# A hybrid decoder trunk on one core: two priorities in the scheduler that orders the instructions

## The chip, the core and the metric

One of the eight cores of a Trainium2 chip runs the whole program. Its engines work side by side, each through its own instructions in a fixed order: TensorE (PE) for matrix products, VectorE (DVE), ScalarE (ACT), GpSimd (POOL), and SyncE (SP), which here only issues DMAs. An instruction that waits for another engine holds everything behind it on its own engine. The metric is the device time of one execution in microseconds, lower is better.

## The reference, cut to what matters

Two layers over 256 tokens of width 1024, all in float32:

```
h = rmsnorm(x, norm_mix)
aq, ak, av, iq, ik, iw, hq, hf, hi, hg, ga, gb = split(h @ w_in)
y_attn = dsa_attention(rope(rmsnorm(aq)), rope(rmsnorm(ak)), av, rope(iq), rope(ik), iw)   # top 64 of 256 keys by an indexer score
o      = hgrn2_chunked(silu(hq), 1 - f, hi, log f)          # f from sigmoid(hf)
y_hgrn = rmsnorm(o) * silu(hg)
merged = sigmoid(ga) * (y_attn @ w_proj_attn) + sigmoid(gb) * (y_hgrn @ w_proj_hgrn)
x = x + merged @ w_out
g, u = split(rmsnorm(x, norm_ffn) @ w_ffn_in)
x = x + (silu(g) * u) @ w_ffn_out
```

The weights are read once. The result is x after the second layer.

## The kernel before

**Products.** A product in float32 is made of three in a shorter format. Each operand is split into a rounded part hi and the rest lo, and hi·hi, hi·lo and lo·hi are added up in PSUM (`mm3`). All weights come in 69 chunks per layer, nearly all of 128 x 2048 elements (1 MB). `take()` fetches the next one: a DMA on SP into a tile w, ACT writes hi as a rounded copy, DVE writes lo = w - hi. There are three buffers each for w, hi and lo, so a chunk's hi can begin once the chunk three before it has been used up by PE. A group of 512 output columns (`group`) takes two such chunks and 48 products of 128x512.

**Order of a layer.** The groups of `w_in` come as idx, aq, ak, hf, hq, av, vh, hg, ga, gb, ga, gb. In between lies the vector work of the attention: `ev_idx` and the top-64 search (eight rounds of MAX and MATCH_REPLACE for each of two blocks of 128 queries, i = 0 and 1, on the tile `work`), `ev_qk` (norm and rotation of queries and keys, tiles raw, sq, s, n.., ropet, rot, then a transpose by PE into `qkp` and a copy by ACT into qT or kT), the logits (`lg`, PE), softmax (`lm`, DVE and ACT), and transposes of it (`ptp`, PE). `ev_hf` sends the forget gate through a transpose on PE (`hfp`) and two sigmoids on ACT (fT, KR). After that come the HGRN part (`hd`, `hl`, `hc`, `po`), both projections (`pj`), `out_gemm` for `w_out` (accumulators wo), the gated product (`fi`), and `out_gemm` for `w_ffn_out` (fo).

**`out_gemm`.** The last two chunks are taken together. The four accumulators (token block i, column half g) then end one after another, 12 products each. Behind each: x = x + accumulator (DVE), and `norm_half`: xg = x·g (DVE), four transposes (`xT`, PE), hi on ACT, lo on DVE (tiles h2T, or hT for the next layer), squares on ACT. `norm_scale` turns the sums of squares into 1/rms by Newton steps on DVE, ten tiny instructions per block.

**What sets the order.** Nothing runs where it is written. Every call is recorded, and `Program.schedule` sorts them by simulating the engines in Python with prices for each instruction. An engine that is free takes, of the instructions that could start, the one with the largest `o.tail + o.extra`: the tail is the longest remaining path in ns, the extra is `prog.rank` at the time of recording. So a rank of 2e4 counts like 20 us more of path. The warm-up products (`gate`, of which `WARM` are recorded) have an extra of -1e9 and fill PE's idle time only; the tile `zero` that they read keeps its buffer (tag s2, six buffers for all temporary tiles) until the last of them. All instructions are emitted by one line, so the profile gives line 467 to all of them, and one tells them apart by their tiles.

Of the kernel before, what the change touches and what calls it, by code (L numbers as in the profile page):

```python
# [26 lines left out]
N_IDX = 324  # L27
C_HQ, C_HF, C_HV, C_HG, C_GA, C_GB = 1860, 2372, 2884, 3396, 3908, 4932
FIRST = {(0, C_IDX): 2, (0, C_AQ): 2}
WARM = 28  # L30
LEVELS = (2, 4, 8)
TWO_PI = 2.0 * np.pi

# [444 lines left out]
def hybrid_trunk(prog, x_d, pos_d, w_in, w_pa, w_ph, w_out, n_mix, n_ffn,  # L478
# [7 lines left out]
    def big(name, shape, dt=F32):  # L486
        return prog.tile("s4", shape, dt, name)
# [4 lines left out]
    def small(name, n=16):  # L492
        return prog.tile("sm", [n], F32, name)

    def bank(name, tag="Q"):
        return prog.tile(tag, [512], F32, name)
# [21 lines left out]
                                     for o in (0, DFF)]) + ([4, 512],))  # L518
        add_rows(w_fo, l, 2, 1024, 0)

    state = {"used": 0}

    def take():
        c = state["used"]
        state["used"] += 1
        a, b, kn = chunks[c]
        k, n = kn or b
        wt, ht, lt = "w" if k * n > 1024 else "s4", "hi", "lo"
        w = prog.tile(wt, [k, n], F32, f"w{c}")
        hi = prog.tile(ht, [k, n], F32R, f"hi{c}")  # L530
        lo = prog.tile(lt, [k, n], F32R, f"lo{c}")
        prog.rank = 5e5 - 1e3 * c
        if kn is None:
            SP.dma_start(w, a)
        else:
            SP.dma_start(w[:, :, 0:256], a)
            SP.dma_start(w[:, :, 256:512], b)
        prog.rank = 0.0
        S.activation(hi, w, AF.Copy)
        V.tensor_tensor(lo, w, hi.bitcast(F32), op=ALU.subtract)  # L540
        return hi, lo

    def mm3(acc, h, hk, wc, wk, wsl, start, stop):

        hh, hl = h
        wh, wl = wc
        with prog.one(main=True):
            PE.matmul(acc, hh[:, hk, :], wh[:, wk, wsl], start=start, stop=False)
            PE.matmul(acc, hh[:, hk, :], wl[:, wk, wsl], start=False, stop=False)
            PE.matmul(acc, hl[:, hk, :], wh[:, wk, wsl], start=False, stop=stop)  # L550
# [32 lines left out]
    gate = bank("gate")  # L583
    for _ in range(WARM):
        PE.matmul(gate[:, 0:256], zero[:, 0:128], zero, start=True, stop=True)
# [15 lines left out]
    def split_to(hi_ap, lo_ap, src, scale=None):  # L601

        if scale is None:
            S.activation(hi_ap, src, AF.Copy)
            V.tensor_tensor(lo_ap, src, hi_ap.bitcast(F32), op=ALU.subtract)
        else:
            S.activation(hi_ap, src, AF.Copy, scale=scale)
            V.scalar_tensor_tensor(lo_ap, src, scale, hi_ap.bitcast(F32), op0=ALU.mult, op1=ALU.subtract)
# [11 lines left out]
    def norm_half(i, g, gkey, hT, ssq, tag):  # L620

        xs = x[:, i, g * 512:(g + 1) * 512]
        pt = bank(f"xT{i}{g}", tag)
        pv = pt.rearrange("p (k t) -> p k t", k=4)
        xg = tmp(f"xg{i}{g}", [512])
        V.tensor_tensor(xg, xs, gbc[gkey][:, g * 512:(g + 1) * 512], op=ALU.mult)
        transpose4(pt, xg)
        split_to(hT[i][0][:, g * 4:g * 4 + 4, :], hT[i][1][:, g * 4:g * 4 + 4, :], pv)
        junk = tmp(f"sq{i}{g}", [512])
        S.activation(junk, xs, AF.Square, accum_out=ssq[:, g:g + 1])  # L630

    def norm_scale(ssq, name):
        t = small(name + "t")
        V.tensor_tensor(t[:, 0:1], ssq[:, 0:1], ssq[:, 1:2], op=ALU.add)
        return newton(t[:, 0:1], 1, 1.0 / D, name)
# [117 lines left out]
    def layer(l, hT, R):  # L753
        last = l == DEPTH - 1
        def group(n, name, evac, kk=4):
            accs = [bank(f"{name}{i}_{l}", "P") for i in range(NT)]
            for c in range(8 // kk):
                wc = take()
                for i in range(NT):
                    for k in range(kk):  # L760
                        kt = c * kk + k
                        mm3(accs[i][:, :n], hT[i], kt, wc, k, slice(0, n), kt == 0, kt == 7)
            for i in range(NT):
                evac(i, accs[i][:, :n])
# [76 lines left out]
        group(512, "ak", ev_qk(1, kT))  # L841


        PT = []
        for i in range(NT):
            W = (i + 1) * 128
            mx, nb, sm, rs = small(f"mx{i}"), small(f"nb{i}"), small(f"sum{i}"), small(f"rs{i}")
            pts = [big(f"PT{i}{j}", [8, 128]) for j in range(i + 1)]
            lms = [big(f"lm{i}{p}", [4, W]) for p in range(2)]
# [13 lines left out]
            for p in range(2):  # L863
# [10 lines left out]
                for j in range(i + 1):  # L874
# [5 lines left out]
                    S.activation(dst, pt.rearrange("p (a t) -> p a t", a=4), AF.Copy)  # L880
            PT.append(pts)

# [41 lines left out]
        for i in range(NT):  # L924
            py = bank(f"py{i}")
            for hp0 in (0, 2):
                with prog.one():
                    for hp in range(hp0, hp0 + 2):
                        for j in range(i + 1):
                            for p in range(2):  # L930
                                h = 2 * hp + p
                                PE.matmul(py[64 * p:64 * p + 64, hp * 128:(hp + 1) * 128], av[:, j, h * 64:(h + 1) * 64],
                                          PT[i][j][:, h, :], start=j == 0, stop=j == i)
            split_to(yT[i][0][:, 0:4, :], yT[i][1][:, 0:4, :], py.rearrange("p (k t) -> p k t", k=4))
# [134 lines left out]
            split_to(yT[i][0][:, 4:8, :], yT[i][1][:, 4:8, :], pv, gc)  # L1069


        gates = {}

        def ev_gate(key):
# [11 lines left out]
        for g in range(2):  # L1086
            ws = [take(), take()]
            for i in range(NT):
                pab = []
                for s in range(2):  # L1090
                    acc = bank(f"pj{s}{i}{g}", "P")
                    for k in range(4):
                        mm3(acc, yT[i], s * 4 + k, ws[s], k, slice(0, 512), k == 0, k == 3)
                    pab.append(acc)
                ma, mb = tmp(f"ma{i}", [512]), tmp(f"mb{i}", [512])
                V.tensor_tensor(ma, pab[0], gates["a" + str(g)][:, i, :], op=ALU.mult)
                V.tensor_tensor(mb, pab[1], gates["b" + str(g)][:, i, :], op=ALU.mult)
                V.tensor_tensor(ma, ma, mb, op=ALU.add)
                pt = bank(f"mp{i}", "Q")
                transpose4(pt, ma)  # L1100
                split_to(mT[i][0][:, g * 4:g * 4 + 4, :], mT[i][1][:, g * 4:g * 4 + 4, :], pt.rearrange("p (k t) -> p k t", k=4))

        def out_gemm(n_chunks, lhs, gkey, hT_out, name):

            accs = [[bank(f"{name}{i}{g}", "Q") for g in range(2)] for i in range(NT)]
            for c in range(n_chunks - 2):
                wc = take()
                for i in range(NT):
                    for k in range(2):
                        (hh, hl), hk = lhs(i, 2 * c + k)  # L1110
                        with prog.one(main=True):
                            for g in range(2):
                                gs = slice(g * 512, (g + 1) * 512)
                                PE.matmul(accs[i][g], hh[:, hk, :], wc[0][:, k, gs], start=c == 0 and k == 0, stop=False)
                                PE.matmul(accs[i][g], hh[:, hk, :], wc[1][:, k, gs], start=False, stop=False)
                            for g in range(2):
                                gs = slice(g * 512, (g + 1) * 512)
                                PE.matmul(accs[i][g], hl[:, hk, :], wc[0][:, k, gs], start=False, stop=False)
            wcs = [take(), take()]
            Rn = []  # L1120
            for i in range(NT):
                ssq = small(f"{name}ss{i}")
                for g in range(2):
                    for c in range(2):
                        for k in range(2):
                            kt = 2 * (n_chunks - 2 + c) + k
                            h, hk = lhs(i, kt)
                            mm3(accs[i][g], h, hk, wcs[c], k, slice(g * 512, (g + 1) * 512), kt == 0, c == 1 and k == 1)
                    xs = x[:, i, g * 512:(g + 1) * 512]
                    V.tensor_tensor(xs, xs, accs[i][g], op=ALU.add)  # L1130
                    if hT_out is not None:
                        norm_half(i, g, gkey, hT_out, ssq, "P")
                    else:
                        SP.dma_start(out_d[0, i * 128:(i + 1) * 128, g * 512:(g + 1) * 512], xs)
                if hT_out is not None:
                    Rn.append(norm_scale(ssq, f"{name}r{i}"))
            return Rn

        h2T = pair(f"h2T{l}")
        R2 = out_gemm(4, lambda i, k: (mT[i], k), f"f{l}", h2T, "wo")  # L1140
        if not last:
            load_g(f"m{l + 1}", n_mix[l + 1])
# [19 lines left out]

        hT_n = None if last else pair(f"hT{l + 1}")
        R_n = out_gemm(11, lambda i, k: ((acts[k // 2][:, i, 0], acts[k // 2][:, i, 1]), k % 2), f"m{l + 1}", hT_n, "fo")
        return hT_n, R_n

    for l in range(DEPTH):
        hT, R = layer(l, hT, R)
# [43 lines left out]
```

## Time and profile before

| | |
|---|---|
| time, median of 3 runs | 814.75 us (814.44 to 815.56) |
| the profiled execution | 815.19 us, of which its span is 813.4 us |
| PE busy | 801.3 us (99%), 3986 products |
| PE weight loads | 657.3 us (81%) |
| DVE busy | 537.6 us (66%) |
| ACT busy | 400.9 us (49%) |
| bytes from HBM | 137.95 MB, 171 GB/s over the span |
| mean granted clock of PE | 0.996 of full speed |

The ends of products are modelled, so a PE that is busy for 99% may still run below its pace. One sees that by the starts: in an undisturbed stretch there are 46 products of 128x512 in 10 us. The chain that ended last lies on PE for 84% and on DVE for 10%, of which the splits (lo) are 4% of the span.

### The profile page before, as it was taken

To read this page: it belongs to the slowest core of one execution; us is meant where nothing else is said; L and a number is where in the kernel's file an instruction comes from. 1 tells how busy PE (TensorE), PEld (TensorE's weight loads), DVE (VectorE), ACT (ScalarE), POOL (GpSimd) and SP (SyncE) were. 2 spreads that over 40 slices of the span, in tenths; PEclk is the share of its full clock that TensorE was granted. 3 is DMA by queue.
4 is the path that set the end of the run, shared out by engine and by line. 5 is a ranking of instruction groups with operands and counts; after the bars stand their busy time and mean duration, and the time that the engine had idled before them with its cause. 6 is when DMAs were issued, how large, how long until landed. Compare 5 with 4: busy or idle time off the path is not lost.

```text
span 813.4 us, 10251 instructions
## 1 busy us (share of the span) xinstructions
PE 801.3 (99%) x3986; PEld 657.3 (81%) x3986; DVE 537.6 (66%) x936; ACT 400.9 (49%) x506; POOL 6.5 (1%) x8
## 2 busy tenths in 40 slices
PE   8989999999999999999999999999999999999998
PEld 7767788888888888888887778888888888888886
DVE  6999856577775455554489997566868645556442
ACT  5764855344364435453356667533445544445330
POOL 3000000000000000000000000000000000000000
PEclk9998999999999999999999999999999999999999
DMA  9725555333656656536546356443354665655531
GB/s 319 248 69 176 186 188 174 104 124 129 219 176 206 195 169 203 170 144 222 168 154 219 111 201 207 155 156 105 108 202 156 206 204 168 199 177 186 169 142 52
DMA packets 86793, 139.66 MB, mean 172 GB/s; under 512 B 3269, under 2 KB 51033, under 8 KB 86745
## 3 DMA queue, kind: packets, MB, share of 16 engines
q1 hardware_dynamic: 86584, 138.94, 51.4%
q8 instruction: 31, 0.51, 0.2%
q14 instruction: 18, 0.14, 0.0%
q10 hardware_dynamic: 160, 0.07, 0.0%
HBM read 137.95 MB, written 1.05 MB: 171 GB/s over the span
## 4 chain that ended last, share of the span: by engine, by line
PE 84%; DVE 10%; issue 2%; ACT 2%; DMA 0%; POOL 0%; POOLq 0%; ACTq 0%; DVEq 0%
PE fi L467 29%; PE fo L467 15%; PE pj L467 5%; PE gb L467 5%; PE wo L467 5%; PE ga L467 4%; DVE lo L467 4%; PE av L467 3%; PE hg L467 3%; PE vh L467 3%; PE hq L467 2%; DVE work L467 2%; PE aq L467 1%; ACT hi L467 1%; PE fp L467 1%
## 5 line engine op out<-in xcount | busy, mean ns | idle before, releaser
L467 DVE TENSOR_TENSOR lo<-w,hi 128x2048 fp32r<-128x2048 f32 (+3 forms) x134 | 296.4, 2212 | 218.5 <-ACT hi L467 217.9
L467 ACT ACTIVATE hi<-w 128x2048 fp32r<-128x2048 f32 (+3 forms) x134 | 247.3, 1846 | 280.7 <-PE fi L467 95.1
L467 PE MATMUL fi<-hi,h2T_hi 128*128 128x512 f32 x352 | 140.8, 400 | 0.2
L467 PE MATMUL fi<-hi,h2T_lo 128*128 128x512 f32 x352 | 137.8, 391 | 0.0
L467 PE MATMUL fi<-lo,h2T_hi 128*128 128x512 f32 x352 | 137.1, 390 | 0.0
L467 PE MATMUL fo<-hi,act 128*128 128x512 f32 x352 | 109.9, 391 | 0.0
L467 PEld LDWEIGHTS fi<-hi,h2T_lo 128*128 128x128 f32 x352 | 66.1, 188 | 15.0 <-DVE h2T_lo L467 0.7
L467 PEld LDWEIGHTS fo<-hi,act 128*128 128x128 f32 x352 | 66.1, 188 | 13.7
L467 PEld LDWEIGHTS fi<-hi,h2T_hi 128*128 128x128 f32 x352 | 66.1, 188 | 13.3 <-DVE h2T_lo L467 0.8
L467 PEld LDWEIGHTS fi<-lo,h2T_hi 128*128 128x128 f32 x352 | 66.2, 188 | 12.6
L467 PE MATMUL fo<-lo,act 128*128 128x512 f32 x176 | 68.5, 389 | 0.0
L467 PEld LDWEIGHTS fo<-lo,act 128*128 128x128 f32 x176 | 33.1, 188 | 6.6
L467 PE MATMUL gb<-hi,hT_hi 128*128 128x512 f32 x64 | 26.7, 418 | 0.0
L467 PE MATMUL wo<-hi,mT_hi 128*128 128x512 f32 x64 | 25.9, 405 | 0.0
L467 PE MATMUL pj<-hi,yT_hi 128*128 128x512 f32 x64 | 25.8, 404 | 0.0
L467 PE MATMUL ga<-hi,hT_hi 128*128 128x512 f32 x64 | 25.7, 401 | 0.0
L467 PE MATMUL wo<-lo,mT_hi 128*128 128x512 f32 x64 | 25.1, 392 | 0.0
L467 PE MATMUL gb<-hi,hT_lo 128*128 128x512 f32 x64 | 25.1, 392 | 0.0
L467 PE MATMUL gb<-lo,hT_hi 128*128 128x512 f32 x64 | 25.0, 391 | 0.0
L467 PE MATMUL ga<-hi,hT_lo 128*128 128x512 f32 x64 | 25.0, 391 | 0.0
L467 PE MATMUL pj<-hi,yT_lo 128*128 128x512 f32 x64 | 25.0, 391 | 0.0
L467 PE MATMUL pj<-lo,yT_hi 128*128 128x512 f32 x64 | 25.0, 390 | 0.0
(340 smaller groups left out, 1302.0 us busy)
## 6 DMA issues: line engine op xcount, KB each, us to landing
w<-in_w_ffn_in_dram SPq DMA_DIRECT2D x88, 512.0 KB, 4.5
w<-in_w_in_dram SPq DMA_DIRECT2D x42, 1024.0 KB, 4.9
w<-in_w_ffn_out_dram SPq DMA_DIRECT2D x22, 1024.0 KB, 4.7
w<-in_w_out_dram SPq DMA_DIRECT2D x8, 1024.0 KB, 4.7
w<-in_w_proj_attn_dram SPq DMA_DIRECT2D x4, 1024.0 KB, 4.9
w<-in_w_proj_hgrn_dram SPq DMA_DIRECT2D x4, 1024.0 KB, 4.8
w<-in_w_in_dram SPq DMA_DIRECT2D x4, 512.0 KB, 4.6
w<-in_w_in_dram SPq DMA_DIRECT2D x4, 324.0 KB, 5.5
```

The costliest lines, as they stand in the source:

```text
L467: getattr(engines[o.eng], name)(*[real(x) for x in a], **{n: real(x) for n, x in k.items()})
```

## The change

```diff
-WARM = 28
+WARM = 24
+AHEAD = 2e4
...
-    state = {"used": 0}
+    state = {"used": 0, "ahead": 0.0}
...
-        prog.rank = 0.0
+        prog.rank = state["ahead"]
         S.activation(hi, w, AF.Copy)
         V.tensor_tensor(lo, w, hi.bitcast(F32), op=ALU.subtract)
+        prog.rank = 0.0
...
         group(512, "ak", ev_qk(1, kT))
+        state["ahead"] = AHEAD
...
             split_to(yT[i][0][:, 4:8, :], yT[i][1][:, 4:8, :], pv, gc)
+        state["ahead"] = 0.0
...
+                    prog.rank = AHEAD
                     xs = x[:, i, g * 512:(g + 1) * 512]
                     V.tensor_tensor(xs, xs, accs[i][g], op=ALU.add)
                     if hT_out is not None:
                         norm_half(i, g, gkey, hT_out, ssq, "P")
                     else:
                         SP.dma_start(out_d[0, i * 128:(i + 1) * 128, g * 512:(g + 1) * 512], xs)
+                    prog.rank = 0.0
```

From the group hf up to hg, both halves of the split of a weight chunk get 20 us of priority. In `out_gemm` the addition to x, the scaled copy, its transposes, its split and the squares get the same. Four warm-up products are dropped. No computation changes; PE has four products fewer, ACT loads its function table 14 times where it did 10 times, SP swaps one small load (the vector for the FFN's norm) with a weight chunk.

VectorE, layer 0, around the split of the first chunk of hq (`lo_800` before, `lo_669` now; work is the top-64 search, n00 the Newton steps of the first query block's norm, ropet a key's rotation). Before:

```order
L467 TENSOR_TENSOR n00a<-n00a,n00v 128x8
L467 TENSOR_TENSOR ropet<-raw_622,rs_775 128x8x32
L467 SCALAR_TENSOR_TENSOR n00y<-n00a,n00y 128x8
L467 TENSOR_TENSOR lo_800<-w_516,hi_648 128x2048
L467 SCALAR_TENSOR_TENSOR n00a<-n00y 128x8
L467 MAX m_812<-work_580 128x8
```

And now:

```order
L468 SCALAR_TENSOR_TENSOR work_630<-rel_628,iw_490,work_630 128x256
L468 MATCH_REPLACE work_606<-m_653,work_606 128x128
L468 MAX m_660<-work_630 128x8
L468 MAX m_667<-work_606 128x8
L468 TENSOR_TENSOR lo_669<-w_520,hi_641 128x2048
L468 MATCH_REPLACE work_606<-m_667,work_606 128x128
L468 MATCH_REPLACE work_630<-m_660,work_630 128x256
```

The split stood behind the whole search but two rounds and behind most of the query norm, as the 153rd instruction of VectorE; now it stands at the beginning of the search, as the 109th. 44 instructions have gone behind it, none has come ahead of it.

TensorE, layer 0, from the end of the group hf to the start of hq (hfp: transposes of the forget gate, qkp: of a rotated query or key). Before:

```order
L467 MATMUL qkp_750<-ident,rot_718 128x128 x4
L467 MATMUL hf_0_687<-hi_578,hT_hi_214 128x512
L467 MATMUL hf_0_687<-lo_694,hT_hi_214 128x512
L467 MATMUL hf_0_687<-hi_578,hT_lo_230 128x512
...
L467 MATMUL hfp_777<-ident,hfraw_748 128x128 x4
L467 MATMUL hfp_804<-ident,hfraw_796 128x128 x4
L467 MATMUL hq_0_815<-hi_648,hT_hi_206 128x512
L467 MATMUL hq_0_815<-lo_800,hT_hi_206 128x512
```

And now, first at the same place and then where the first hfp has gone, in the group vh:

```order
L468 MATMUL hf_0_673<-lo_587,hT_hi_215 128x512
L468 MATMUL hf_0_673<-hi_558,hT_lo_231 128x512
L468 MATMUL hq_0_743<-hi_641,hT_hi_207 128x512
L468 MATMUL hq_0_743<-lo_669,hT_hi_207 128x512
...
L468 MATMUL vh_0_1004<-hi_927,hT_lo_221 128x512
L468 MATMUL ptp_1108<-ident,lm_1010 128x128 x4
L468 MATMUL hfp_1114<-ident,hfraw_793 128x128 x4
L468 MATMUL vh_0_1004<-hi_927,hT_hi_207 128x512
```

No transpose stands between hf and hq any more. The second query block's qkp has gone 27 products into hq, both keys' qkp into av and vh, the logits lg from hq and av into av and vh, and the second hfp right behind the first transpose of hq's own gate, in the first group gb. Layer 1 is moved likewise.

TensorE, end of the product with `w_out` (wo_2031 before and wo_2028 now are the last accumulator, i = 1 and g = 1; 12 products each). Before:

```order
L467 MATMUL wo_2030<-hi_2050,mT_lo_1998 128x512
L467 MATMUL xT_2122<-ident,xg_2102 128x128 x4
L467 MATMUL wo_2031<-hi_1970,mT_hi_1985 128x512
...
L467 MATMUL wo_2031<-hi_1970,mT_lo_1998 128x512
L467 MATMUL xT_2145<-ident,xg_2109 128x128 x4
L467 MATMUL wo_2031<-hi_2050,mT_hi_1985 128x512
...
L467 MATMUL xT_2164<-ident,xg_2135 128x128 x4
L467 MATMUL fi_2173<-hi_2063,h2T_hi_2132 128x512
```

And now:

```order
L468 MATMUL xT_2110<-ident,xg_2099 128x128 x4
L468 MATMUL xT_2119<-ident,xg_2106 128x128 x4
L468 MATMUL wo_2027<-hi_2047,mT_hi_1982 128x512
...
L468 MATMUL xT_2161<-ident,xg_2151 128x128 x4
L468 MATMUL fi_2170<-hi_2060,h2T_hi_2126 128x512
...
L468 MATMUL fi_2170<-hi_2060,h2T_lo_2135 128x512
L468 MATMUL xT_2186<-ident,xg_2177 128x128 x4
L468 MATMUL fi_2170<-hi_2060,h2T_hi_2126 128x512
```

The first two transposes come three and nine products earlier, and the fourth, which came behind 27 products of fi, comes behind six.

## Rows read from the trace of the kernel before

**Rows 1.** Windows: us, busy us (instructions) of PE, PEld, DVE, ACT, POOL, PEclk, DMA
```profile
50.00:60.00 10.00, 6.73 (x34) 4.96 (x33) 10.00 (x34) 7.38 (x9) 0.00 (x0) 0.98 0.32 106
60.00:70.00 10.00, 9.68 (x32) 7.71 (x33) 10.00 (x46) 2.70 (x5) 0.00 (x0) 0.67 0.46 141
240.00:250.00 10.00, 10.00 (x46) 8.28 (x45) 5.37 (x4) 5.79 (x5) 0.00 (x0) 1.00 0.55 186
```

**Rows 2.** Timeline of PE, layer 0: start, us, operation [idle before <-releaser]
```profile
26.64 0.51 PE L467 MATMUL ak<-lo,hT_hi 128*128 128x512 f32 x1 [0.16 <-DVE lo L467]
...
53.00 0.39 PE L467 MATMUL hf<-hi,hT_lo 128*128 128x512 f32 x1
53.56 0.63 PE L467 MATMUL qkp<-ident,rot 128*128 128x128 f32 x4 [0.17 <-DVE rot L467]
53.94 0.48 PE L467 MATMUL hf<-hi,hT_hi 128*128 128x512 f32 x1
...
55.41 0.60 PE L467 MATMUL hfp<-ident,hfraw 128*128 128x128 f32 x4
58.16 0.66 PE L467 MATMUL hfp<-ident,hfraw 128*128 128x128 f32 x4 [2.14 <-ACT hfraw L467]
58.57 0.47 PE L467 MATMUL hq<-hi,hT_hi 128*128 128x512 f32 x1
60.32 0.79 PE L467 MATMUL hq<-lo,hT_hi 128*128 128x512 f32 x1 [1.28 <-DVE lo L467]
...
66.46 0.44 PE L467 MATMUL hq<-hi,hT_hi 128*128 128x512 f32 x1
```

**Rows 3.** Timeline of DVE, layer 0
```profile
46.91 2.27 DVE L467 TENSOR_TENSOR lo<-w,hi 128x2048 fp32r<-128x2048 f32 x1
49.10 0.08 DVE L467 MATCH_VALUE_LOAD work<-m,work 128x8 f32 x1
...
57.98 2.29 DVE L467 TENSOR_TENSOR lo<-w,hi 128x2048 fp32r<-128x2048 f32 x1
...
67.24 0.69 DVE L467 TENSOR_TENSOR rot<-rot,n10y 128x512 f32<-128x512 f32 x1
```

**Rows 4.** DVE groups by form, 24.3 to 58 us: busy us, mean ns, idle before
```profile
L467 DVE MAX8 m<-work 128x8 f32<-128x256 f32 x8 | 3.3, 416 | 0.0
L467 DVE MATCH_REPLACE8 work<-m,work 128x256 f32<-128x256 f32 x8 | 3.3, 407 | 0.0
L467 DVE TENSOR_TENSOR rot<-raw,rc 128x512 f32<-128x512 f32 x3 | 2.0, 678 | 0.0
```

**Rows 5.** Timeline of PE, layer 1
```profile
417.63 0.51 PE L467 MATMUL aq<-lo,hT_hi 128*128 128x512 f32 x1 [0.17 <-DVE lo L467]
...
459.45 0.50 PE L467 MATMUL hq<-lo,hT_hi 128*128 128x512 f32 x1 [0.18 <-DVE lo L467]
...
465.12 0.48 PE L467 MATMUL hq<-hi,hT_hi 128*128 128x512 f32 x1
465.87 0.50 PE L467 MATMUL hq<-lo,hT_hi 128*128 128x512 f32 x1 [0.26 <-DVE lo L467]
```

**Rows 6.** Timeline of PE behind the first product with w_out
```profile
229.15 0.50 PE L467 MATMUL fi<-hi,h2T_lo 128*128 128x512 f32 x1
229.74 0.50 PE L467 MATMUL fi<-hi,h2T_hi 128*128 128x512 f32 x1
```

**Rows 7.** Timeline of ACT, layer 0
```profile
58.12 1.28 ACT L467 ACT_TABLE_LOAD   x1
59.41 0.60 ACT L467 ACTIVATE fT<-hfp 128x512 f32<-128x512 f32 x1
```

**Rows 8.** Timeline of DVE, layer 1, in the first group gb
```profile
531.05 0.18 DVE L467 TENSOR_TENSOR F<-F 128x16 f32<-128x16 f32 x1 [2.58 <-PE hqp L467]
531.93 2.29 DVE L467 TENSOR_TENSOR lo<-w,hi 128x2048 fp32r<-128x2048 f32 x1 [0.70 <-ACT hi L467]
```

## Prediction

> **What bounds the kernel now.** I read the windows first, by the number of products that PE starts in 10 us, because its busy time is modelled. At rest 46 products of 128x512 start in 10 us, 0.227 us apart from start to start, with DVE busy for half of the time [rows 1]. From 50 to 60 us only 34 instructions start, from 60 to 70 us 32, and there DVE is busy for all of both stretches [rows 1]. So for most of the time PE's own stream is the bound, and nothing that these priorities move can shorten it; around layer 0's attention it is DVE. Then I went through PE's timeline for every place where the next start comes later than 0.227 us (0.38 us behind a set of four transposes, the step from 53.56 to 53.94 [rows 2]). What PE could win back is the list of these places, and I found no others that the change touches:
> - layer 0, one wait for a split at 26.64 us, 0.41 us from start to start above the normal step;
> - layer 0, 53.00 to 60.32 us: qkp comes 0.33 us late, the second hfp 2.75 us behind the first instead of 0.38 (2.37 lost), and hq's first product with lo 1.75 us behind its predecessor (1.52 lost) [rows 2]. Together with the first wait 4.6 us;
> - 60.32 to 66.46 us: 14 steps in 6.14 us, where 14 times 0.227 are 3.18, so 2.96 us lost. The granted clock from 60 to 70 us is 0.67 of full speed [rows 1], a mixture of the two levels 1.2 and 2.4 GHz. PE had stood almost still from 55.8 to 60.3 us just before. These steps are the second half of the price of that stop;
> - layer 1: three waits for a split, 0.17, 0.18 and 0.26 us long. The last one costs 0.52 us from start to start (0.75 less 0.227), so 0.26 us beyond the wait itself; for the three I take 1.3 us [rows 5];
> - behind each product with w_out: 0.59 us between two starts instead of 0.227, so 0.36 us lost, and 0.72 us in both layers [rows 6].
>
> The chain behind the large one: hq's first split began at 57.98 us [rows 3], though its hi was there long before, because it stood in DVE's queue behind the top-64 search. The hfp in front of it on PE was late only because ACT's copy of hf was late; PE would have had nothing to do without it, since lo was missing until 60.2 us.
>
> **The change part by part.**
>
> *Splits ahead in the attention.* DVE has no idle time between 24.3 and 58 us [rows 4], so a split's start is the sum of what stands ahead of it. Of the instructions ahead of hq's first split, 44 have moved behind it and none has come ahead. Starts on DVE lie about 0.08 us closer together than durations say (the split of 46.91 us lasts 2.27, the next instruction starts 2.19 later [rows 3]). So a MAX8 of 256 costs 0.33 us and a replacement of 256 with its load 0.41 [rows 4]; half of the MAX8 and five of the replacements are on 128 columns, which I take at 0.20 and 0.27. That makes 11 MAX8 3.0 us and 13 replacements 4.6 us; seven 512-wide or four-times-half-wide pieces of rotation and sums (0.60 us each by [rows 4], the halves 0.34) 4.4 us; eleven tiny ones 0.8 us. Together 12.8 us: the split starts at 45.2 instead of 57.98 us and is done at 47.4. PE needs it behind hf, which now ends at 58.57 - 0.41 - 0.33 - 2.37 - 1.2 (two sets hfp and one qkp that no longer stand there) - 0.2 (three warm-up products fewer) = 54.1 us. The margin is 6.7 us. The same count for the following chunks gives margins of 4 to 6 us; a split can't start before the chunk three ahead of it is used up, and then its hi and lo need 4.5 us while PE has two chunks (10.9 us) in hand. So the stops of 4.6 us go, and with them, since PE then runs without a stop, the 2.96 us at the lower clock.
>
> *What is late next.* DVE's work is the same, so the attention now runs later by the splits that have gone ahead. The tightest place is the qkp of the first key block, 36 products into av. On DVE its last rotation stood at 67.24 us [rows 3]; three more splits (6.6 us) and 0.1 us of small work now stand ahead of it, 0.75 us have gone behind it. So 73.2, done at 73.8, and with the 0.2 us that a releaser takes here 74.0 us. PE is there at 54.1 + 84 x 0.227 + 0.38 = 73.6 us. A wait of 0.4 us in layer 0. In layer 1 the same sum gives 0.5 us. The other products that wait for the attention (second qkp, lg, ptp) come out within 0.5 us of DVE, mostly on the right side. ACT copies the second half of hf out of PSUM only behind the split copies now, and av's second accumulator needs that bank: 0.3 us. Were there no such waits at all it would be 1.2 us less, and were DVE 2 us later everywhere than I count, some 3 us more in the two layers.
>
> *Function tables.* ACT loads one 14 times instead of 10. A load takes 1.28 us and the next activation starts 1.29 us behind its start [rows 7], so 5.2 us more on an engine that is busy for half of the span; the fullest place is the softmax of the second query block, where a load stands ahead of four exponentials and PE's transposes wait for them. I count about 0.6 us of margin there, so nothing. The Trainium skill (ScalarE: Activation LUTs, What ACT_TABLE_LOAD costs) gives 1283 ns for the load and about 1380 ns of drain for each change of set, 2.66 us together, and says to group calls by set; the trace agrees with the load and shows no drain beside it. By the page the transposes would come 0.8 us late in each layer and my sum would be 1.6 us higher.
>
> *Forget gate later.* The second hfp, its two sigmoids and the products F now come in the first group gb. F is 1.5 us on DVE, in layer 1 eight small scalings (1.0 us) come with it. DVE is idle there for 2.58 and 0.70 us, once behind the first transposes and once ahead of the next split [rows 8]; the layer-0 copy of this place looks the same. So nothing; without this cover up to 2.5 us per layer at hd.
>
> *Residual and norm first.* The wait behind w_out goes (0.72 us in both layers): the third transposes' lo no longer stands behind a split of 2.2 us. The fourth xT now comes only six products of fi behind the end of wo, 1.8 us with the third set; x and xg need two DVE steps of 0.61 (a 512-wide instruction as at 67.24 [rows 3]) and three releases, about 1.9 to 2.1 us. I take 0.3 us of wait in each layer, from 0 to 0.6. The split that goes behind comes 1.3 us later; it has 2.7 us until PE needs it. Were that gone, 2 us. At the end of the first fo the same, and its wait is already in layer 1's 1.3. The last fo keeps its order: 0.
>
> *Warm-up products and the load on SP.* 0.2 us for products of 0.04 to 0.15 us, already used in part above. Their real effect is that tile zero's buffer is free some 40 us earlier. SP's swapped DMA: nothing, its queue waits for split buffers there.
>
> **Sum.** 4.6 + 2.96 + 1.3 + 0.72 + 0.2 = 9.8 us to win back, less 0.4 + 0.5 + 0.3 + 0.6 = 1.8 us of new waits: 8.0 us. The profiled execution took 815.19 us, so 807.2; the median of the runs is 0.44 us lower, so **806.7 us**.
>
> **The rivals.**
> 1. *PE waits for the attention instead of the splits.* The four products with a margin below 0.5 us speak for it, and DVE at 10.00 of 10 us [rows 1]: any idle time that the new order forces on DVE comes on top. Against it: the instructions are the same, and the three buffers hold the splits back to PE's pace. At 2 us of lag in each layer, 3 to 4 us of the gain go: 809 to 811.5 us.
> 2. *It gives everything back later,* so that it doesn't do what it is said to: the attention's end, not the splits, sets when the projections can start. DVE is then full until about 106 us instead of 97, and PE wants the last softmax transposes at about 114 us, a margin of 8 us, and DVE is idle in gb [rows 8]. That speaks against it. If it held, 814 to 815 us.
> 3. *Slower: the stop comes back in two places.* If DVE is 4 us later than I count at the key's rotation, PE stands in av as long as it stood ahead of hq, and the clock falls again as from 60 to 66 us; in both layers that is 2 x (4.5 + 3.0) = 15 us against 9.8 won: about 820 us. It decides from 4 us of lag, that is a rotation done at 78 instead of 74 us. The sum of durations is off by 0.1 us over 34 us where I could hold it against the trace, which speaks against it. The Trainium skill (TensorE: Matmul & The Clock Gate, Part 1) says that an idle PE falls back to half rate and needs sustained work to return; the trace shows it once, at 0.67 from 60 to 70 us, and by that rule layer 1's short waits cost no clock, as they do here.
>
> **How the numbers follow.** Chances: forecast 0.62 (805 to 809 us), rival 1 0.20, rival 2 0.11, rival 3 0.07. The range reaches from no new wait at all (814.75 - 9.8 = 805.0, less 0.4 for steps that I rounded) to the end of rival 1: 804.6 to 811.5 us. About 0.2% (1.6 us) is what a measurement of this kernel can tell from no change, so below 813.1 counts as faster: forecast and rival 1, 0.82, and a little of rival 2; 0.83. Within 0.2% 0.10, slower 0.07.
>
> **What would show it.** In the trace after: 44 or more products in each 10 us from 50 to 70 us and a granted clock of 1.00 there; hq's first lo at about 45 us on DVE; hq starting at about 54 us; the end of hg near 107 us instead of 114.4. A wait of PE at the third qkp in av below 1 us; in rival 1 it is 2 us or more, and lg and ptp have waits too. In gb a wait at hd would show rival 2. Behind wo the step of 0.59 us gone and at most 0.6 us ahead of the fourth xT. I am wrong if DVE stands idle between 24 and 75 us, since all starts on it are sums without gaps.

## The result, and the profile after

The changed kernel takes **805.3 us** (median of 4 runs, 805.24 to 805.91) where the kernel before took 814.88 on the same chip: a ratio of 0.9883 (95% interval 0.9866 to 0.9900), 9.6 us less. The forecast was 806.7 us with a range of 804.6 to 811.5. The profiled execution took 805.24 us, of which its span is 803.4; before it was 815.19 and 813.4. One execution of the experiments, the traced one of e4, ran with a mean granted clock of 0.556 and took 1343.97 us; it is left out of every time below.

The page's first lines show that no engine has less to do. DVE and ACT are busy a little longer than before (537.6 and 400.9 us there), and PE has four products fewer:

```profile
span 803.4 us, 10248 instructions
...
PE 795.3 (99%) x3982; PEld 654.7 (81%) x3982; DVE 539.3 (67%) x936; ACT 405.6 (50%) x510; POOL 5.7 (1%) x8
```

The windows of layer 0's attention (columns as in [rows 1]) have 46 and 47 PE instructions where [rows 1] has 34 and 32, and a granted clock of 1.00 where it was 0.67. DVE is as full as it was, 10.00 of 10 us:

```profile
50.00:60.00 10.00, 10.00 (x46) 8.29 (x45) 10.00 (x24) 3.70 (x4) 0.00 (x0) 1.00 0.50 170
60.00:70.00 10.00, 10.00 (x47) 8.06 (x46) 10.00 (x33) 5.68 (x6) 0.00 (x0) 1.00 0.66 210
```

PE's timeline of after (start, duration, operation, idle time before it). The first four lines answer [rows 2]: hf runs into hq without a pause, in steps of 0.227 us. The next two are the third qkp in layer 0, the last two the same place in layer 1, the only new wait that the profile names in either attention (one of 0.36 us ahead of a product hl is in both kernels, at 149.42 us before and at 141.97 now):

```profile
53.81 0.39 PE L468 MATMUL hf<-hi,hT_lo 128*128 128x512 f32 x1
54.04 0.39 PE L468 MATMUL hq<-hi,hT_hi 128*128 128x512 f32 x1
54.27 0.39 PE L468 MATMUL hq<-lo,hT_hi 128*128 128x512 f32 x1
54.49 0.39 PE L468 MATMUL hq<-hi,hT_lo 128*128 128x512 f32 x1
...
73.51 0.39 PE L468 MATMUL av<-hi,hT_lo 128*128 128x512 f32 x1
73.93 0.63 PE L468 MATMUL qkp<-ident,rot 128*128 128x128 f32 x4
...
461.67 0.39 PE L468 MATMUL av<-hi,hT_lo 128*128 128x512 f32 x1
462.47 0.63 PE L468 MATMUL qkp<-ident,rot 128*128 128x128 f32 x4 [0.42 <-DVE n01a L468]
```

DVE's timeline of after answers [rows 3]: hq's first split begins at 44.94 instead of 57.98 us, the key's last rotation at 73.11 instead of 67.24:

```profile
44.94 2.28 DVE L468 TENSOR_TENSOR lo<-w,hi 128x2048 fp32r<-128x2048 f32 x1
...
73.11 0.68 DVE L468 TENSOR_TENSOR rot<-rot,n10y 128x512 f32<-128x512 f32 x1
```

PE behind the first product with `w_out` (beside [rows 6]): the fourth set of transposes xT now stands six products behind the third, and the steps of fi around it are not stretched:

```profile
219.29 0.39 PE L468 MATMUL fi<-lo,h2T_hi 128*128 128x512 f32 x1
219.51 0.40 PE L468 MATMUL fi<-hi,h2T_lo 128*128 128x512 f32 x1
219.75 0.60 PE L468 MATMUL xT<-ident,xg 128*128 128x128 f32 x4
220.11 0.48 PE L468 MATMUL fi<-hi,h2T_hi 128*128 128x512 f32 x1
```

### The profile page after: what moved, and what is told of

It is laid out like the page before. It is cut to its first block, busy times and chain, and to the rows that moved or that the text cites. A ratio compares the mean times of both kernels' runs of the same rounds, so it can differ in the third digit from the quotient of the medians.

```text
span 803.4 us, 10248 instructions
## 1 busy us (share of the span) xinstructions
PE 795.3 (99%) x3982; PEld 654.7 (81%) x3982; DVE 539.3 (67%) x936; ACT 405.6 (50%) x510; POOL 5.7 (1%) x8
## 4 chain that ended last, share of the span: by engine, by line
PE 91%; DVE 5%; issue 1%; DMA 1%; ACT 1%; SPq 0%; ACTq 0%
PE fi L468 30%; PE fo L468 15%; PE wo L468 5%; PE pj L468 5%; PE gb L468 5%; PE ga L468 4%; PE vh L468 3%; PE aq L468 3%; PE hg L468 3%; PE av L468 3%; DVE lo L468 2%; PE ak L468 1%; PE hq L468 1%; PE hf L468 1%; PE fp L468 1%
```

## The experiments

Where a kernel won is read best from the same product in both traces. The table gives, in us, what each kernel gained on the kernel before between six pairs of marks (starts of products; a minus is a loss): the start up to layer 0's last idx product; from there to the first pj (layer 0's attention); to the last fi of layer 0 (w_out's end); to layer 1's last ak (end of fo, norm); to its first pj (attention); to its last fi.

| kernel | start | attention 0 | w_out 0 | end of fo | attention 1 | w_out 1 |
|---|---|---|---|---|---|---|
| the change | 0.26 | 7.19 | 0.58 | 0.51 | 0.75 | 0.52 |
| e1, splits only | -0.05 | 6.72 | -0.35 | 0.01 | 1.31 | -0.12 |
| e2, output products only | -0.44 | 1.22 | 0.58 | 0.50 | 1.29 | 0.54 |
| e3, warm-up only | 0.41 | 0.40 | -0.11 | 0.00 | 0.10 | -0.11 |
| e6, lag of 2.7 us | 0.32 | 4.42 | 0.56 | 0.59 | -3.59 | 0.53 |
| e7, lag of 5.7 us | -0.34 | -1.14 | 0.59 | 0.50 | -6.46 | 0.58 |
| e8, splits in layer 0 only | -0.23 | 7.23 | 0.58 | 0.51 | 1.27 | 0.62 |
| e10, e8 and hT_lo on VectorE | 1.42 | 6.88 | 0.62 | 0.51 | 1.30 | 0.62 |
| e11, the change again | -0.91 | 7.09 | 0.57 | 0.57 | 0.75 | 0.57 |
| e12, hT_lo on VectorE only | 0.08 | 7.19 | 0.62 | 0.51 | 0.81 | 0.55 |

The start is no property of a kernel: e11 is the changed kernel once more, and its last idx product came 1.17 us later than in the trace above. From the second column on both agree within 0.1 us.

### Which part won what: e1, e2, e3

**e1** is the kernel before with the splits' priority alone:

```diff
-WARM = 24
+WARM = 28
...
-                    prog.rank = AHEAD
+                    prog.rank = 0.0
```

> The kernel before, with the priority of the splits alone (28 warm-up products, no priority at the two output products). Theory A, the forecast's own terms: 4.6 us of stops in layer 0, 2.96 us of half clock, about 1.0 us of layer 1's waits, less 1.2 us of new waits: 7.4 us less than before, about 807.4 us. Theory B, that the changed kernel's trace suggests (the new waits are only 0.2 us in layer 0 and 0.35 us in layer 1): 8.2 to 8.8 us less, 806.0 to 806.6 us, that is nearly all of the 9.6 us that the whole change won. Rival, that the split priorities win only the stops and the clock came back for another reason: 4 to 5 us less, about 810 us.

Measured: 807.43 us against 814.98, ratio 0.9908 (0.9893 to 0.9923), 7.5 us less, which is theory A's number; the whole change had 9.6. Layer 0's attention is 6.72 us of it, for 6.9 by theory A's terms. That the sum agrees as well is partly luck: layer 1's attention wins 1.31 us where those terms leave 0.5, and 0.47 us are lost behind the two w_out. (Most of the -0.35 is a last warm-up product that here stands ahead of the first wo product, at 195.29 us, and makes it 0.5 us late; the wait behind w_out stays as it was.) Building the kernel with the priority on lo alone (hi at rank 0) gives, instruction for instruction, the changed program on every engine. So it is the place on DVE that counts here, and ACT's half of the rank does nothing.

**e2** has the priority at the output products alone:

```diff
-WARM = 24
+WARM = 28
...
-        state["ahead"] = AHEAD
+        state["ahead"] = 0.0
```

> The kernel before, with the priority at the two output products alone. Theory A, the forecast's terms: 0.72 us won behind the two products with w_out, 0.6 us lost ahead of the fourth transposes: 0.1 us less, 814.7 us. Theory B: a late start also makes the steps on both sides of it longer by 0.1 us each, and nothing waits ahead of the fourth transposes: 2 x 0.56, 1.1 us less, 813.7 us; with the end of layer 0's fo another 0.3 to 0.5 us.

Measured: 811.84 us, ratio 0.9963 (0.9950 to 0.9975), 3.1 us less, more than either theory. Behind each w_out it wins 0.54 to 0.58 us (theory B's 0.56). Two gains were in no theory. Layer 1's attention wins 1.29 us: with its first norm earlier, layer 1 has no wait for a split at all, so the splits' priority has nothing left to win there. And layer 0's attention wins 1.22 us, though its instructions stand there as before. PE's timeline of e2 shows why:

```profile
55.86 0.60 PE L468 MATMUL hfp<-ident,hfraw 128*128 128x128 f32 x4
58.60 0.66 PE L468 MATMUL hfp<-ident,hfraw 128*128 128x128 f32 x4 [2.14 <-ACT hfraw L468]
...
60.76 0.50 PE L468 MATMUL hq<-lo,hT_hi 128*128 128x512 f32 x1 [1.27 <-DVE lo L468]
61.09 0.39 PE L468 MATMUL hq<-hi,hT_lo 128*128 128x512 f32 x1
61.32 0.40 PE L468 MATMUL hq<-hi,hT_hi 128*128 128x512 f32 x1
...
66.10 0.39 PE L468 MATMUL hq<-hi,hT_hi 128*128 128x512 f32 x1
67.82 0.50 PE L468 MATMUL hq<-lo,hT_hi 128*128 128x512 f32 x1 [1.33 <-DVE lo L468]
```

The stop is that of [rows 2], 2.14 and 1.27 us, but this time the clock was not lowered behind it: the steps from 61.09 on are 0.23 us, not 0.43, and the window from 60 to 70 us has a granted clock of 1.00. What PE won by that, it mostly lost behind 66.10 us, where it waited for hq's second split. In the kernel before that wait does not show, because the half rate hides it: DVE wrote that split from 65.04 to 67.33 us, and PE came for it only at 68.81. DVE and then PE of the kernel before:

```profile
65.04 2.29 DVE L467 TENSOR_TENSOR lo<-w,hi 128x2048 fp32r<-128x2048 f32 x1
```

```profile
68.81 0.39 PE L467 MATMUL hq<-lo,hT_hi 128*128 128x512 f32 x1
```

The 1.22 us belong to the traced execution and not to the median. Of e2's five executions it alone has a mean granted clock of 1.000; the other four have 0.995 to 0.997 and took as long (811.5 to 812.2 us, the traced one 811.77), and the traced one lost 0.44 us at the start. Without these two columns the table's gains are 2.9 us.

**e3** has 24 warm-up products and nothing else:

```diff
-WARM = 28
+WARM = 24
```

> The kernel before with 24 warm-up products instead of 28, nothing else. By the forecast 0.2 us less, 814.6 us, with the stop ahead of hq as before. Rival: the buffer of the tile zero, free 40 us earlier, lets the vector work of the first 30 us go earlier, and the stop ahead of hq gets shorter by a microsecond or more: 813 us or less.

Measured: 814.06 us, ratio 0.9991 (0.9982 to 1.0000). The traced execution won 0.69 us (814.50 against 815.19). Of that 0.41 lie in the start, which varies by more from one execution to the next; behind it 0.27 us are left, and the stop ahead of hq stayed (2.14 and 2.06 us). That fits the forecast's 0.2 us, and the rival, a shorter stop, did not happen.

The three medians add up to 7.5 + 3.1 + 0.9 = 11.6 us, 2.0 more than the whole change. The table says where: in layer 1's attention e1 and e2 win 1.31 and 1.29 us by taking away the same waits, and together only 0.75. (e2's 1.22 us in layer 0 lie in e1's 6.72 too, but they are no part of its median.)

### What the half clock cost: e4, e5, e9

The forecast counted 2.96 us for 14 steps at half rate. To see that price by itself, the stop was filled with repeated products, so that the split comes late but PE does not stand still. In **e4** and **e5** (the same kernel twice; the trace is e5's) the first pause got ten repetitions of hq's first product and the second pause six:

```diff
+        extra.calls = [same] * 10
+        self.order.insert(at, extra)      # ahead of the second hfp
+        hq.calls = [same] * 6 + hq.calls
```

> The kernel before in its own order, with the stop ahead of hq in layer 0 filled: TensorE repeats hq's first product 10 times ahead of the second hfp and 6 times behind it (each repetition starts the accumulation anew, so the sum is the same). The split comes as late as before, and nothing else moves. Theory A (the half rate after the stop is the price of TensorE standing still): granted clock 1.00 from 60 to 70 us, the products from 60.3 us on start 0.227 us apart, and the time is 2.9 us shorter, about 811.9 us; the stop itself stays. Rival (the steps of 0.43 us have another cause, such as transfers or late operands): the clock stays at 0.67 there and the time within 0.5 us of before.

> The kernel of e4 once more, for a trace at the usual clock. Theory A (the half rate is a price of its own): an execution in which the clock is not lowered is 2.9 us shorter than before. Theory C, from e2's trace: with the clock held, TensorE arrives at hq's second chunk before its split is done (at 67.3 us on VectorE), so a wait of about 1.5 us at the 25th product of hq takes the place of the half rate, and the time stays within 0.5 us of before (814.5 to 815 us).

Measured: e4 815.6 us (before 814.98), e5 816.52 (815.31), ratios 1.0010 (1.0001 to 1.0019) and 1.0009 (0.9998 to 1.0020). The fill did not do its work: the first repetition waited 2.14 us like the hfp that it stood ahead of. In e5 ACT wrote hq's hi only from 56.07 to 57.98 us, and the profile puts the release down to hfraw, which follows it on ACT and ended at 58.56; why the repetition waited for that one too is not shown. e5's timeline:

```profile
55.87 0.60 PE L482 MATMUL hfp<-ident,hfraw 128*128 128x128 f32 x4
58.61 4.14 PE L482 MATMUL hq<-hi,hT_hi 128*128 128x512 f32 x10 [2.14 <-ACT hfraw L482]
62.58 0.60 PE L482 MATMUL hfp<-ident,hfraw 128*128 128x128 f32 x4
```

The ten repetitions took 3.97 us instead of 2.27: the clock fell while they ran, after one pause only. The other executions differ in this. Eight of the 18 of e4 and e5 have a mean granted clock of 0.999 or 1.000 and took 814.8 to 815.2 us; the other ten have 0.997 or 0.998 and took 816.1 to 817.3. Between the means lie 1.7 us, which is what the ten repetitions lost: with no wait for a split behind them the half rate is paid in full. That the first eight are hardly faster than the kernel before says little, since the 16 repetitions are 3.6 us of work for PE. The kernel before says more. Beside e1 to e12 it ran 56 times: 33 executions with a clock of 0.996 took 815.3 us in the mean, 20 with 0.997 or 0.998 took 814.4, and three with 1.000 took 814.6. So a clock that stays up is worth well under 2.96 us there, but the start varies too much for a number.

**e9** fills the first pause with six more copies of the first hfp's transposes, whose operands are there:

```diff
+        tr.calls = tr.calls * 7           # the first hfp
+        hq.calls = [same] * 6 + hq.calls
```

> The kernel before in its own order, the stop ahead of hq in layer 0 filled once more: the first hfp's four transposes are repeated 6 times in the first pause (in e4 and e5 the fill there had itself waited 2.14 us for hq's hi), hq's first product 6 times in the second. Every repetition writes the same values. Theory A (the half rate has a price of its own, 2.96 us): granted clock 1.00 from 60 to 70 us and 2.9 us less, about 812 us. Theory C: granted clock 1.00, but a wait of 1.3 to 1.5 us ahead of the 25th product of hq, and the time 0 to 1.3 us below before, 813.7 to 815 us. Theory E (TensorE's standing still is not what lowers the clock here): it stays near 0.67 there although TensorE has no pause, and the time is that of before or above it.

Measured: 815.71 us against 814.62, ratio 1.0013 (1.0004 to 1.0022). All 11 executions have a mean granted clock of 0.999 or 1.000, so theory E falls: with the pauses filled the clock stays up. Theory A's 812 us fails too. Window and timeline of the traced one:

```profile
60.00:70.00 10.00, 7.47 (x33) 5.28 (x32) 10.00 (x36) 3.42 (x5) 0.00 (x0) 1.00 0.32 105
```

```profile
55.45 3.66 PE L476 MATMUL hfp<-ident,hfraw 128*128 128x128 f32 x32
58.86 1.87 PE L476 MATMUL hq<-hi,hT_hi 128*128 128x512 f32 x7
61.97 0.50 PE L476 MATMUL hq<-lo,hT_hi 128*128 128x512 f32 x1 [1.24 <-DVE lo L476]
...
69.03 0.50 PE L476 MATMUL hq<-lo,hT_hi 128*128 128x512 f32 x1 [1.29 <-DVE lo L476]
```

The clock is 1.00 from 60 to 70 us and every step 0.23, and the wait for the second split is there, 1.29 us. The repeated transposes had a side effect: they hold a temporary buffer that DVE needs, DVE stood for 1.51 us, and hq's first split began at 59.63 us, 1.65 later than before; so the time lies above theory C's 813.7 to 815 us. Yet hq ended only 0.42 us later (its last product at 76.53 instead of 76.11). If the end of hq moves with its splits, the held clock gave 1.65 - 0.42 = 1.23 us. e2 gives the same: split 0.43 us later, end of hq 0.80 earlier, 1.23 us. That is what the half rate cost by itself in these two traces, 1.2 of the 2.96 us. The other 1.7 us are a wait for hq's second split, hidden in the trace before.

### How near the new order is to a wait: e6, e7

Rivals 1 and 3 were tested by force: idle DVE instructions (a 512-wide product of zeros) ahead of the first key block's rotation, in both layers, four in **e6** and eight in **e7**. They were meant to take 0.6 us each and took 0.69, one every 0.73 us. The key's last rotation in layer 0 came at 75.77 and 79.41 us instead of 73.11; less what the start moved, the lag is 2.7 us in e6 and 5.7 in e7:

```diff
+        v = self.lagv
+        extra.calls = [("tensor_tensor", (v, v, v), {"op": ALU.mult})] * n     # n = 4, 8
+        self.order.insert(k, extra)       # ahead of the first rot10 of each layer
```

> The changed kernel with 4 idle VectorE instructions of 0.6 us (2.4 us) ahead of the rotation of the first key block, in both layers; nothing else moves. Forecast's rival 1 (2 us of lag in each layer cost 3 to 4 us): 808.5 to 809.5 us. Theory C (each microsecond of lag is a microsecond of waiting at the third qkp, since that wait is already there in both layers, and is not made up later): 2 x 2.4 = 4.8 us more, 810.1 us. Theory D (the lag is taken up in VectorE's idle time further on): below 807 us.

> The same with 8 such instructions (4.8 us) at both places. Forecast's rival 3 (a stop of 4 us or more brings the half clock with it, 3 us for each): 2 x (4.8 + 3.0) = 15.6 us more, about 821 us. Theory C (only the stop counts; where the clock falls, it hides a wait for VectorE that would stand there anyway): 2 x 4.8 = 9.6 us more, about 815 us, with or without a lower granted clock behind the stop.

Measured: e6 812.29 us, ratio 0.9963 (0.9948 to 0.9978); e7 820.64, ratio 1.0055 (1.0037 to 1.0074). The spans are 7.0 and 16.1 us above the changed kernel's. The 820.64 us agree with rival 3's price, about 820 us in the forecast and 821 in the expectation, but with more lag than its 4 us; with the lag as it came, the expectation's sum is 2 x (5.7 + 3.0) = 17.4 us against the 16.1 measured. Theory C is too low in both: 5.4 and 11.4 us with the lag as it came, against 7.0 and 16.1. In layer 0 the wait is also at another place than I had named. PE of e6, then ACT of e6:

```profile
68.50 0.39 PE L479 MATMUL av<-hi,hT_lo 128*128 128x512 f32 x1
71.53 0.50 PE L479 MATMUL av<-hi,hT_hi 128*128 128x512 f32 x1 [2.65 <-ACT hqraw L479]
```

```profile
69.63 0.69 ACT L479 ACTIVATE hfraw<-hf,r1y 128x512 f32<-128x512 f32 x1 [2.14 <-DVE ropet L479]
70.79 0.69 ACT L479 ACTIVATE hqraw<-hq,r0y 128x512 f32<-128x512 f32 x1 [0.47 <-DVE rot L479]
```

av's second accumulator needs a PSUM bank that is free only when ACT has copied out an older accumulator. Those copies (hfraw, hqraw) wait for buffers that DVE's rotations still hold. In the changed kernel this product starts at 68.85 us, 0.03 us behind its normal step, so there is no margin here; in e10 and e12 below it waits 0.27 and 0.29 us. The third qkp, which I took for the tightest place, comes 5 us later and in layer 0 did not wait longer in e6 than in the change. In layer 1 it waited 2.12 us in e6, and the steps behind it are stretched to 0.43:

```profile
467.91 0.63 PE L479 MATMUL qkp<-ident,rot 128*128 128x128 f32 x4 [2.12 <-DVE n01a L479]
...
469.87 0.63 PE L479 MATMUL av<-hi,hT_lo 128*128 128x512 f32 x1
470.30 0.63 PE L479 MATMUL av<-hi,hT_hi 128*128 128x512 f32 x1
```

e7 has, in layer 0, the bank and a split late, and then the half clock:

```profile
71.12 0.50 PE L479 MATMUL av<-lo,hT_hi 128*128 128x512 f32 x1 [1.97 <-DVE lo L479]
71.46 0.40 PE L479 MATMUL av<-hi,hT_lo 128*128 128x512 f32 x1
75.16 0.80 PE L479 MATMUL av<-hi,hT_hi 128*128 128x512 f32 x1 [3.31 <-ACT hqraw L479]
75.76 0.63 PE L479 MATMUL av<-lo,hT_hi 128*128 128x512 f32 x1
76.18 0.63 PE L479 MATMUL av<-hi,hT_lo 128*128 128x512 f32 x1
```

2.1 + 3.5 us of stops, then 13 stretched steps up to 80.9 us, one by 0.37 and twelve by 0.2 us: 2.8 us. Here the half rate is paid in full, since no later wait stands behind it. The sum is 8.4 us; the table's step from 7.19 to -1.14 is 8.3.

### A faster version: e8, e10, e12

**e8** gives the splits priority in layer 0 alone, since e2's layer 1 had no wait left:

```diff
-        state["ahead"] = AHEAD
+        state["ahead"] = AHEAD if l == 0 else 0.0
```

> The changed kernel, but the splits go first in layer 0 alone; in layer 1 their order is the one of e2, the priority at the output products stays. From e2's trace: with that priority alone layer 1 has no wait for a split left and gains 2.3 us from its start to the end of its attention, where the changed kernel gains 1.8 us. Theory B (in layer 1 both priorities remove the same waits, and the splits' priority adds the wait of 0.57 us at the third qkp): 0.5 us less than the changed kernel, 804.8 us. Rival (the splits' priority is what removes layer 1's waits): 1 us more, 806.3 us.

Measured: 805.26 us, ratio 0.9874 (0.9859 to 0.9889); the change has 0.9883. In the trace layer 1's attention wins 1.27 us instead of 0.75, as theory B has it, and the third qkp there no longer waits. The times don't show it: the two intervals overlap. The traces do: from the second column of the table on, the change and e11 agree within 0.1 us, and e8 wins 0.52 us more than both in layer 1's attention.

**e10** also moves the three `hT_lo` of the start from GpSimd to VectorE; **e12** does that alone, beside the change itself (**e11**):

```diff
-            E = V if g == 0 and i == 0 else POOL
+            E = V
```

> The kernel of e8 with one more step, a try at a faster version: the three lower halves of the transposed input (hT_lo) that GpSimd writes at the start go to VectorE. In the changed kernel's trace TensorE waits for them 0.68 and 0.40 us at 12.6 and 14.7 us. If VectorE has room there (it is busy for 4.5 of the first 10 us and 9.2 of the next): 0.5 to 1.1 us less than e8, about 804.3 us. Rival (VectorE is full from 16 us on, and three instructions of 0.6 us go into the attention's tight place, the third qkp): 805.3 us or more.

> The changed kernel itself, beside e12 on one chip, so that the version of e10 and the change can be held against each other. 805.3 us, with 0.4 us either way for the chip.

> The changed kernel with the three hT_lo on VectorE and nothing else (splits first in both layers). e10's trace gains 1.1 us by the first 20 us, loses 0.2 in layer 0's av, and gains 0.6 in layer 1. If each of its two steps stands for itself: 0.9 us less than e11, about 804.4 us, and e10's other 0.6 us belong to layer 1. Rival: the whole of e10's gain comes from the start: 803.4 us.

Measured: e10 803.35 us, ratio 0.9865 (0.9852 to 0.9879), the fastest kernel here; e11 805.83, ratio 0.9886 (0.9871 to 0.9901); e12 805.33, ratio 0.9880 (0.9864 to 0.9897). e12 is 0.5 us below e11, on the same chip, but their runs overlap (805.17 to 805.41 and 805.06 to 806.39). Of e10's 1.42 us in the start the edit explains a part at most: e12 makes the same start in the same order, and its last idx product came at 17.42 us, e10's at 16.08, but its first idx product too came 1.54 us later (9.66 and 8.12). From the first to the last, idx took 7.76 and 7.96 us in these two, and 8.25 to 9.00 in e8, e11 and the change. e10 beats the kernel before by 1.35%. That it beats the change is not shown: the intervals overlap. In the traces layer 1's attention speaks for it (1.30 us, e12 0.81), as it does for e8.

## Why the prediction held, point by point

| term | forecast, us | measured, us |
|---|---|---|
| start and layer 0's attention | 4.6 + 2.96 + 0.2 - 0.4 - 0.3 = 7.1 | 0.26 + 7.19 = 7.45 |
| behind w_out, each layer | 0.36 - 0.3 = 0.06 | 0.58 and 0.52 |
| end of fo and layer 1's attention | 1.3 - 0.5 = 0.8 | 0.51 + 0.75 = 1.26 |
| sum | 8.0 | 9.8, with the end of the span 10.0 |

- **The stops in layer 0 went, for the reason given.** The split was forecast at 45.2 us and hq's start at 54.1; they came at 44.94 and 54.04. The key's rotation was forecast at 73.2 and came at 73.11. The sums of durations on a full DVE held to 0.3 us over the 28 us between these two. DVE, whose idling would have refuted the forecast, was busy for all 51.00 us from 24 to 75.
- **The term of 2.96 us had the right size and more than half the wrong name.** The half clock itself was worth 1.2 us (e2, e9); the rest was a wait for hq's second split, which the half rate had hidden and which the same priority removes. That the one change removes both is luck of the forecast: for a change that only held the clock, this term would have been 1.7 us too large. I read the stretched steps as lost time without asking what PE would have met at full rate.
- **New waits were mis-sized:** 1.8 us in the forecast. Measured, the third qkp has 0.19 us in layer 0 (for 0.4) and 0.57 in layer 1 (for 0.5), the bank of av 0.03, or 0.14 with the step behind it (for 0.3), the fourth xT no wait (for 0.3 in each layer). I had taken the middle of a bound of 0 to 0.6 there. This is the largest part of the 1.6 us by which the forecast of 8.0 us stayed below the 9.6 measured.
- **The wait behind w_out was mis-sized the other way.** I counted the one step of 0.59 us, 0.36. The steps on both sides of it are also stretched, 0.33 and 0.34 us from start to start, so that it cost 0.58; that is what left (0.58 and 0.52). The kernel before, around [rows 6]:

```profile
228.82 0.39 PE L467 MATMUL fi<-lo,h2T_hi 128*128 128x512 f32 x1
...
230.08 0.40 PE L467 MATMUL fi<-lo,h2T_hi 128*128 128x512 f32 x1
```

- **Function tables:** nothing, as forecast. Each of the 14 loads of after takes 1.28 us, and the next activation starts 1.29 or 1.30 us behind its start. The Trainium skill (ScalarE: Activation LUTs, What ACT_TABLE_LOAD costs) adds a drain of about 1380 ns; this trace shows none here either.
- **Rival 1** did not happen, but by less than I thought: I put 3 to 4 us on 2 us of lag in each layer, which is 4 to 5.4 on the 2.7 us of e6, and e6 lost 7.0.
- **Rival 2** did not happen. hg ended at 106.6 us (forecast 107), and the gain at the first pj is still there.
- **Rival 3** had the mechanism right, a stop and the half rate behind it in both layers, and its price was met at more lag than it named (e7: 820.64 us at 5.7 us of lag). The half rate also comes below 4 us: with 2.7 us of lag layer 1 already shows steps of 0.43 us behind a stop of 2.1.

## To carry to other kernels

A split or another preparation that a full in-order engine does for PE should go ahead of vector work that nobody waits for yet; add up the durations that it passes, and then look for the next product that waits for what was pushed back, the release of buffers and PSUM banks included. Two priorities that each remove the same wait don't add up, so try each alone and per stage: here the traces say that one of them was better left out in layer 1 (0.5 us, which the times can't tell). Before counting slow steps as lost time, work out where the engine would have waited next at full speed.

## What the runs showed of the hardware

- **The same stop lowered the clock in one execution and not in another.** PE stood 2.14 and 1.28 us before ([rows 2]), and the granted clock fell to 0.67 for 60 to 70 us; in e2 it stood 2.14 and 1.27 us at the same two instructions, and it stayed at 1.00. e2's other executions have a mean clock of 0.995 to 0.997, and of the 56 executions of the kernel before three have 1.000; with the pauses filled (e9) all 11 stay at 0.999 or 1.000. In e5 one pause of 2.14 us was enough: ten products without a pause between them took 3.97 us instead of 2.27. The Trainium skill (TensorE: Matmul & The Clock Gate, Part 1) says that an idle PE falls to half rate; e5 and e7 agree, e2 shows that a stop alone does not decide it.
- **What the half rate costs depends on what stands behind it.** The same 0.2 us a step cost 1.23 of 2.96 us where the next operand was late as well (e2, e9), and all of it, 2.8 us in e7 and 1.7 in e5, where no wait stood behind.
- **A short wait on PE stretches the step behind it.** At the six waits of 0.3 to 0.5 us in the kernel before (26.64, 229.74, 417.63, 459.45, 465.87 and 627.02 us) the next step is 0.33 or 0.34 us instead of 0.227, and behind both w_out the step ahead of the wait is 0.33 as well. There 0.2 us are lost that no wait in the profile accounts for.
- **The start varies by more than small edits bring:** the last idx product of layer 0 came at 17.24 and at 18.41 us in two executions of the same program.
